# Entry of a gate and up stage: operand sums moved from GpSimd to VectorE, finer layer norm steps, two more early chunks

## The chip, the core and the metric

One NeuronCore of a Trainium2 chip runs the kernel. The metric is the device time in microseconds (us), as the median of several executions. The engines are called PE (TensorE), DVE (VectorE), ACT (ScalarE), POOL (GpSimd) and SP (SyncE); all transfers here are issued from SP's queue.

## The reference

One layer of a decoder on 1024 new prompt tokens and 8 sequences of 4 sample tokens, 1056 tokens in all, in fp32:

```python
m = W_out(concat[gated_delta_net_heads(x), sliding_window_attention_heads(x)])
x = layernorm(ALPHA * x + m)                       # layer norm 1
gate, up = split(x @ w_ffn_in)
x = layernorm(ALPHA * x + (silu(gate) * up) @ w_ffn_out)
```

The model width is 1024. The states and key and value caches are outputs too. The change touches the end of layer norm 1 and the first of the two products of the SwiGLU, here called the gate and up stage.

## The kernel before, in words

Activations lie transposed in SBUF: 8 tiles of 128 partitions (d = 0 to 7) by tokens, in two halves of 512 and 544 columns. An fp32 product is made of three matmuls on parts in fp32r: every operand is split into a high part, a copy by ACT, and a low part, the raw value minus the high part, by DVE. `product` (L1796 to L1798) runs wh·xh, wh·xl and wl·xh for four tiles. Weights are loaded in pieces of 128x512 (256 KB) and split at L161 (wh, ACT) and L162 (wl, DVE); four split pieces are held at a time.

The hidden width is 22 chunks (f = 0 to 21) of 128 gate and 128 up columns. A chunk is made by seven products in place of eight (the Strassen-Winograd scheme). Weights of a chunk are quarters A11, A12, A21, A22; operands are B11 and B21 (first half of the tokens, d 0 to 3 and d 4 to 7) and B12 and B22 (second half, 544 wide). With T1 = B12 - B11, T2 = B22 - T1, T3 = B22 - B12 and T4 = B21 - T2, and weight sums S1 to S4 that POOL makes for each chunk (L1625, L1626, L1630, L1636; tiles named S), PE runs in this order: A11·B11, S2·T2, A12·B21, S3·T3, A22·T4, S1·T1, S4·B22.

A11·B11 (`head`: ACT copies it out to x1 at L1857) and A12·B21 (`head2`: ACT's Silu to x2 at L1865) need only the first half. So the first NE = 10 chunks run these two products early, while the other engines finish the second half's layer norm 1 and the operands T. Eight of these chunks store x1 and x2 in DRAM and read them back when their turn comes. Then PE waits until all operands are there (`need(lambda: "T" in flags)`) and the loop over f runs the other products.

The second half's layer norm is two groups of 272 columns (named l11 and l12). It multiplies by 1/sigma at L1531 (DVE) or, for two tiles of each group, L1529 (POOL), applies weight and bias at L1532 (ACT), and splits B22 in pieces of 272 columns at once (L1694 and L1695). `combine` makes the sums for four tiles i: T1 on POOL (L1730), T3 on DVE (L1731), T2 in T1's place on DVE (L1735), T4 in T3's place on POOL (L1736), each split right after it.

The program is written as generators that hand over to each other (`spawn`, `pump`, `need`, `yield`). A scheduler with its own timeline then sets each engine's order, and every engine runs its list in order. A buffer taken from the pool is first written by a tiny memset on POOL (L228), which waits until the slot's last reader is done; POOL's list stands still until then.

## Time and profile before

| | |
|---|---|
| median of 3 runs | 1309.69 us (1306.21 to 1312.10) |
| profiled execution | 1308.84 us |
| its span | 1307.0 us |
| PE busy in the span | 1249.6 us (96%) |
| DVE, ACT, POOL busy | 887.3, 620.2, 393.4 us |
| chain that ended last | PE 79%, DVE 10%, ACT 3%, issue 3%, DMA 3%, POOL 2% |

The profile is of one execution, 0.85 us under the median; 1.84 us of it lie outside the span. Matmuls overlap, so a matmul's own duration (0.39 us for 512 columns) is longer than the distance from its start to the next one's start, and that distance is the price. Tile names in the rows are without buffer numbers: "T1raw" at L1735 is T2, "T3raw" at L1736 is T4, "x" at L1857 an x1 tile. The early chunks and the entry lie between 505 and 640 us, the loop over the chunks after that.

### The profile page before, as it was taken

To read this page: it belongs to the slowest core of one execution; us is meant where nothing else is said; L and a number is where in the kernel's file an instruction comes from. 1 tells how busy PE (TensorE), PEld (TensorE's weight loads), DVE (VectorE), ACT (ScalarE), POOL (GpSimd) and SP (SyncE) were. 2 spreads that over 40 slices of the span, in tenths; PEclk is the share of its full clock that TensorE was granted. 3 is DMA by queue.
4 is the path that set the end of the run, shared out by engine and by line. 5 is a ranking of instruction groups with operands and counts; after the bars stand their busy time and mean duration, and the time that the engine had idled before them with its cause. 6 is when DMAs were issued, how large, how long until landed. Compare 5 with 4: busy or idle time off the path is not lost.

```text
span 1307.0 us, 25072 instructions
## 1 busy us (share of the span) xinstructions
PE 1249.6 (96%) x8673; PEld 1126.6 (86%) x8673; DVE 887.3 (68%) x2040; ACT 620.2 (47%) x1376; POOL 393.4 (30%) x1207
## 2 busy tenths in 40 slices
PE   8999899989899998997899999999999999999996
PEld 6877689988899987985899999999999999788995
DVE  6787975887986777868856665555555765632674
ACT  7765644656755542577322223223333554622453
POOL 1009410205713133436744332332321112111210
PEclk9999999999999998998899999999999999999998
DMA  7431341242223545545454432222323886643461
GB/s 256 130 89 66 89 134 46 87 127 65 62 83 125 170 142 163 180 135 192 143 156 140 142 108 75 90 70 78 104 91 101 279 284 187 201 121 108 142 220 47
DMA packets 119103, 170.82 MB, mean 131 GB/s; under 512 B 20272, under 2 KB 50096, under 8 KB 118960
## 3 DMA queue, kind: packets, MB, share of 16 engines
q1 hardware_dynamic: 118976, 169.22, 41.3%
q8 instruction: 68, 1.11, 0.3%
q14 instruction: 59, 0.48, 0.1%
HBM read 138.44 MB, written 31.75 MB: 130 GB/s over the span
## 4 chain that ended last, share of the span: by engine, by line
PE 79%; DVE 10%; ACT 3%; issue 3%; DMA 3%; POOL 2%; SPq 0%; DVEq 0%; ACTq 0%; POOLq 0%
PE acc L427 6%; PE acc L428 6%; PE acc L426 6%; PE acc L1796 6%; PE acc L1797 6%; PE acc L1798 6%; PE acc L1967 6%; PE acc L1965 6%; PE acc L1966 6%; PE ms L1798 5%; PE ms L1796 5%; PE ms L1797 5%; DMA hr<-hd 1%; DVE wl L162 1%; DVE st L1063 1%
## 5 line engine op out<-in xcount | busy, mean ns | idle before, releaser
L162 DVE TENSOR_TENSOR wl<-wr,wh 128x512 fp32r<-128x512 f32 x330 | 242.2, 737 | 143.5 <-ACT wh L161 137.4
L161 ACT CAST wh<-wr 128x512 fp32r<-128x512 f32 x330 | 197.5, 602 | 261.2 <-PE acc L1966 104.2
L426 PE MATMUL acc<-xh,wh 128*128 128x272 f32 (+1 forms) x528 | 174.9, 331 | 6.0 <-ACT xh L345 5.2
L427 PE MATMUL acc<-xl,wh 128*128 128x272 f32 (+1 forms) x528 | 174.0, 330 | 0.0
L1967 PE MATMUL acc<-hx,wl 128*128 128x272 f32 (+1 forms) x528 | 171.8, 326 | 2.0 <-DVE wl L162 2.0
L428 PE MATMUL acc<-xh,wl 128*128 128x272 f32 (+1 forms) x528 | 173.6, 329 | 0.0
L1965 PE MATMUL acc<-hx,wh 128*128 128x272 f32 (+1 forms) x528 | 172.5, 327 | 1.0 <-ACT wh L161 1.0
L161 ACT CAST wh<-S 128x512 fp32r<-128x512 f32 x88 | 54.4, 619 | 148.0 <-PE acc L1797 96.3
L426 PEld LDWEIGHTS acc<-xh,wh 128*128 128x128 f32 x528 | 100.8, 191 | 13.2 <-ACT xh L345 5.2
L1967 PEld LDWEIGHTS acc<-hx,wl 128*128 128x128 f32 x528 | 99.9, 189 | 11.3 <-DVE wl L162 3.3
L1965 PEld LDWEIGHTS acc<-hx,wh 128*128 128x128 f32 x528 | 99.8, 189 | 9.7 <-POOL hx L228 1.2
L427 PEld LDWEIGHTS acc<-xl,wh 128*128 128x128 f32 x528 | 100.6, 191 | 8.6 <-issue 1.8
L428 PEld LDWEIGHTS acc<-xh,wl 128*128 128x128 f32 x528 | 100.8, 191 | 7.0 <-issue 0.2
L1966 PE MATMUL acc<-hx,wh 128*128 128x272 f32 x352 | 101.9, 290 | 0.0
L162 DVE TENSOR_TENSOR wl<-S,wh 128x512 fp32r<-128x512 f32 x88 | 71.3, 812 | 37.4 <-ACT wh L161 34.7
L1966 PE MATMUL acc<-hy,wh 128*128 128x512 f32 x176 | 69.5, 395 | 0.0
L1966 PEld LDWEIGHTS acc<-hx,wh 128*128 128x128 f32 x352 | 67.0, 191 | 0.3
L428 PE MATMUL acc<-mh,wl 128*128 128x272 f32 (+1 forms) x192 | 63.4, 330 | 0.0
L426 PE MATMUL acc<-mh,wh 128*128 128x272 f32 (+1 forms) x192 | 62.9, 328 | 0.0
L427 PE MATMUL acc<-ml,wh 128*128 128x272 f32 (+1 forms) x192 | 62.5, 326 | 0.0
L1694 ACT CAST hx<-hr 128x272 fp32r<-128x272 f32 (+1 forms) x66 | 31.5, 486 | 52.3 <-DMA hr<-hd 49.8
L1798 PE MATMUL ms<-T2h,wl 128*128 128x272 f32 x176 | 50.8, 289 | 0.0
(629 smaller groups left out, 3481.8 us busy)
## 6 DMA issues: line engine op xcount, KB each, us to landing
wr<-in_w_ffo_t SPq DMA_DIRECT2D x120, 256.0 KB, 2.9
wr<-in_w_ffi_t SPq DMA_DIRECT2D x108, 256.0 KB, 2.8
wr<-in_w_in_t SPq DMA_DIRECT2D x88, 256.0 KB, 2.7
wr<-in_w_out_t SPq DMA_DIRECT2D x32, 256.0 KB, 2.9
hd<-x SPq DMA_DIRECT2D x22, 272.0 KB, 2.8
hr<-hd SPq DMA_DIRECT2D x44, 136.0 KB, 2.7
hd<-x SPq DMA_DIRECT2D x22, 256.0 KB, 2.0
hr<-hd SPq DMA_DIRECT2D x22, 256.0 KB, 4.8
```

What stands on the lines that cost most here:

```text
L161: nc.scalar.copy(hi, raw)
L162: nc.vector.tensor_tensor(lo, raw, hi.bitcast(F32), ALU.subtract)
L426: mm(ps[:, :cw], wh, xh[kt][:, c0:c0 + cw], start=(kt == 0), stop=False)
L427: mm(ps[:, :cw], wh, xl[kt][:, c0:c0 + cw], start=False, stop=False)
L428: mm(ps[:, :cw], wl, xh[kt][:, c0:c0 + cw], start=False, stop=(kt == n - 1))
L1694: A.copy(hi, raw)
L1796: mm(o, wh[:, kt, :], xh, start=(start and kt == 0), stop=False, **kw)
L1797: mm(o, wh[:, kt, :], xl, start=False, stop=False, **kw)
L1798: mm(o, wl[:, kt, :], xh, start=False, stop=(kt == 3), **kw)
L1965: mm(ps, wh[:, f % 4, :], xh, start=(f == 0), stop=False)
L1966: mm(ps, wh[:, f % 4, :], xl, start=False, stop=False)
L1967: mm(ps, wl[:, f % 4, :], xh, start=False, stop=(f == NF - 1))
```

## The change

T1, T2 and T3 get a raw tile each and T4 is written over T2; all four subtractions are on DVE (now L1739, L1740, L1742, L1745), and T2 is made and split first; T3, T4, T1 and B22 are split behind it, with a flag each that the product which needs it waits for. B22 is no longer split in the layer norm but last in `combine`, in whole pieces of 544 columns. The layer norm of the second half hands over after every tile, puts all multiplies on DVE (L1533) and runs its steps with a longer lag (L1F). Twelve chunks are early: ten ahead of the loop as before, chunk 10 between S2·T2 and S3·T3 of chunk 0, and chunk 11 between S3·T3 and A22·T4. In the changed program the split of weights is L163 and L164, the copies to x1 and x2 are L1876 and L1884, and POOL's sums L1627, L1628, L1632 and L1638.

```diff
--- before.py
+++ after.py
@@ -78,11 +78,13 @@
     return c
 
 
-NE = 10
+NE = 12
+NBETWEEN = 2
 NKEEP_X = 2
 PM = (1, 4)
 MID = (1, 4)
 L1 = (0, 1)
+L1F = (1, 3)
 LE = 0
 BUDS = (2750.0, 3000.0)
 IDLE = (9, 4, 2, 3, 2, 4)
@@ -1466,7 +1468,7 @@
         hook(1)
 
 
-    def layernorm(tiles, ssum, cw, gi, nm, done, lag=(0, 0), sums=None, bk="acc", order=range(8)):
+    def layernorm(tiles, ssum, cw, gi, nm, done, lag=(0, 0), sums=None, bk="acc", order=range(8), fine=False):
 
 
         def ones_mm(src):
@@ -1502,7 +1504,7 @@
                 else:
                     G.tensor_tensor(v[0], v[0], q, ALU.add)
                 drop()
-            if i % 2 and not sums:
+            if (i % 2 or fine) and not sums:
                 yield 0.0
         drop(bk)
         if not sums:
@@ -1525,13 +1527,13 @@
         drop()
         for j, i in enumerate(order):
             t = tiles[i]
-            if j in PM:
+            if j in PM and not fine:
                 G.tensor_tensor(t, t, y, ALU.mult)
             else:
                 pin(V.tensor_tensor(t, t, y, ALU.mult))
             A.activation(t, t, AF.Identity, bias=cols[:, gi + 1, i:i + 1], scale=cols[:, gi, i:i + 1])
             done(i, t)
-            if j % 2:
+            if j % 2 or fine:
                 yield 0.0
         drop()
 
@@ -1643,9 +1645,12 @@
         return {"S2": (s2, first), "S3": (last("S3", f"S3_{f}"), third), "S1": (last("S1", f"S1_{f}"), None),
                 "S4": (last("S2", f"S2_{f}"), None)}
 
-    for f in range(NE):
+    def ahead(f):
         q = quarters(f)
-        plan[f] = {n: W.plain(W.raw(q[n])) for n in ("A11", "A12")}
+        plan.setdefault(f, {}).update({n: W.plain(W.raw(q[n])) for n in ("A11", "A12")})
+
+    for f in range(NE - NBETWEEN):
+        ahead(f)
     for f in range(NF):
         q, early = quarters(f), f < NE
         uses = {"A11": 2 - early, "A21": 1, "A22": 1, "A12": 2 - early}
@@ -1657,6 +1662,8 @@
                 p[n] = W.piece(*sm[n])
             elif n not in p:
                 p[n] = W.plain(r[n])
+            if f == 0 and n in ("S2", "S3"):
+                ahead(NE - 2 + (n == "S3"))
     wfo = I["w_ffo_t"]
     fo = {(g, d): W.whole(wfo[:, d * NF * P:(d + 1) * NF * P]) for g in range(len(GT)) for d in range(8)}
 
@@ -1701,13 +1708,13 @@
 
         def done(i, t):
             dma(out=yd[i][:, SG[s][0] + c0:SG[s][0] + c0 + cw], in_=t)
-            n = {(0, 0): "B11", (0, 1): "B21", (1, 1): "B22"}.get((s, i // 4))
+            n = {(0, 0): "B11", (0, 1): "B21"}.get((s, i // 4))
             if n:
                 split(*(x[:, cs] for x in B[n][i % 4]), t)
             flags.add(("y1", gi, i))
 
-        yield from layernorm([ac[s][d][:, cs] for d in range(8)], ssum, cw, 0, f"l1{gi}", done, L1, bk="acc" if gi else "ms",
-                             order=(0, 4, 1, 5, 2, 6, 3, 7) if s else range(8))
+        yield from layernorm([ac[s][d][:, cs] for d in range(8)], ssum, cw, 0, f"l1{gi}", done, L1F if s else L1,
+                             bk="acc" if gi else "ms", order=(0, 4, 1, 5, 2, 6, 3, 7) if s else range(8), fine=s)
         flags.add(("y1", gi))
 
     def pair(n, i, w, tags=("hp", "xp", "xs")):
@@ -1721,29 +1728,38 @@
 
     def combine():
 
+
+        raws = []
         for i in range(4):
             yield from wait(*[("y1", g, j) for g in range(3) for j in (i, 4 + i)])
             b11, b21, b12, b22 = ac[0][i], ac[0][4 + i], ac[1][i], ac[1][4 + i]
-            while not spare(8):
+            while not spare(5):
                 yield BLOCK
-            t1, t3 = (take([P, HW_], F32, f"{n}raw{i}") for n in ("T1", "T3"))
-            G.tensor_tensor(t1, b12, b11, ALU.subtract)
+            t1, t2, t3 = (take([P, HW_], F32, f"{n}raw{i}") for n in ("T1", "T2", "T3"))
+            V.tensor_tensor(t1, b12, b11, ALU.subtract)
+            V.tensor_tensor(t2, b22, t1, ALU.subtract)
+            yield 0.0
             V.tensor_tensor(t3, b22, b12, ALU.subtract)
-            split(*pair("T3", i, HW_), t3)
+            split(*pair("T2", i, HW_), t2)
             yield 0.0
-            split(*pair("T1", i, HW_), t1)
-            V.tensor_tensor(t1, b22, t1, ALU.subtract)
-            G.tensor_tensor(t3, b21, t1, ALU.subtract)
-            split(*pair("T2", i, HW_), t1)
+            V.tensor_tensor(t2, b21, t2, ALU.subtract)
+            raws.append((t1, t2, t3, b22))
+            drop("hp", 3)
             yield 0.0
-            give(f"T1raw{i}")
-            while not spare(2):
-                yield BLOCK
-            split(*(x[:, 0:512] for x in pair("T4", i, 512)), t3[:, 0:512])
-            give(f"T3raw{i}")
-            drop("hp", 4)
-            yield 0.0
-        flags.add("T")
+        flags.add("T2")
+        for n, j, w in (("T3", 2, HW_), ("T4", 1, 512), ("T1", 0, HW_), ("B22", 3, HW_)):
+            for i in range(4):
+                while not spare(2) and n != "B22":
+                    yield BLOCK
+                p = B[n][i] if n == "B22" else pair(n, i, w)
+                split(*(x[:, 0:w] for x in p), raws[i][j][:, 0:w])
+                if j < 3:
+                    give(f"T{j + 1}raw{i}")
+                else:
+                    drop()
+                if i % 2:
+                    yield 0.0
+            flags.add(n)
 
     def split_mix():
         for t in range(8):
@@ -1780,6 +1796,7 @@
 
 
     HALF = [(0, 272), (272, 544)]
+    filling = [1]
 
     def banks(tag, w):
         n = 1 if w == 512 else 2
@@ -1798,6 +1815,8 @@
                 mm(o, wl[:, kt, :], xh, start=False, stop=(kt == 3), **kw)
                 if c1 - c0 == 512 and kt == 1:
                     W.step()
+                    if filling:
+                        pump(BUD[0])
             if c1 == 272:
                 unit()
 
@@ -1867,13 +1886,16 @@
         unit()
 
     xd = [[k.dp.tile([P, w], F32, name=f"xd{f}_{w}") for w in (HW_, 512)] for f in range(NE)]
-    for f in range(NE):
+    def early(f):
         head(f)
         head2(f)
         if f >= NKEEP_X:
             for i in range(2):
                 dma(out=xd[f][i], in_=X[f][i])
                 give(f"x{i + 1}_{f}")
+
+    for f in range(NE - NBETWEEN):
+        early(f)
 
     def recall(f):
         if NKEEP_X <= f < NE:
@@ -1883,7 +1905,7 @@
             for i in range(2):
                 dma(out=X[f][i], in_=xd[f][i])
 
-    need(lambda: "T" in flags)
+    need(lambda: "T2" in flags)
     for f in range(NF):
         end = f == NF - 1
         p = plan[f]
@@ -1902,10 +1924,13 @@
         unit()
         if f >= NE:
             head2(f)
+        if f == 0:
+            early(NE - 2)
         if end:
             free("B21")
         while not spare(2):
             assert pump(), "no progress"
+        need(lambda: "T3" in flags)
         x3 = take([P, HW_], F32, f"x3_{f}")
         q = banks("acc", HW_)
         product(p["S3"], "T3", q)
@@ -1914,6 +1939,9 @@
         if end:
             free("T3")
         unit()
+        if f == 0:
+            early(NE - 1)
+        need(lambda: "T4" in flags)
         x4 = take([P, 512], F32, f"x4_{f}")
         q = banks("acc", 512)
         product(p["A22"], "T4", q)
@@ -1926,12 +1954,16 @@
         if end:
             free("T4")
         unit()
+        need(lambda: "T1" in flags)
         q = banks("ms", HW_)
         product(p["S1"], "T1", q)
         evac(q, lambda ps, c: V.tensor_tensor(x3[:, c], x3[:, c], ps, ALU.add))
         if end:
             free("T1")
         unit()
+        if f == 0:
+            need(lambda: "B22" in flags)
+            filling.clear()
         product(p["S4"], "B22", q, start=False)
         evac(q, lambda ps, c: V.tensor_tensor(x1[:, c], x1[:, c], ps, ALU.add))
         drop("ms", 2)
```

DVE's list ahead of wl138, the low part of the weights of the last early A11·B11, before (wl137 and wl138 are weights, T1l and T3l low parts of operands, T1raw at L1735 is T2):

```order
L162 TENSOR_TENSOR wl137_8110<-wr137_7779,wh137_8109 128x512
L1695 TENSOR_TENSOR T1l0_7923<-T1raw0_7872,T1h0_7921 128x544
L1695 TENSOR_TENSOR B22l2_6871<-mx16_4283,B22h2_6869 128x272
L1695 TENSOR_TENSOR T3l1_8027<-T3raw1_8021,T3h1_8025 128x544
L1695 TENSOR_TENSOR T1l1_8058<-T1raw1_8019,T1h1_8056 128x544
L1735 TENSOR_TENSOR T1raw0_7872<-mx14_3540,T1raw0_7872 128x544
L162 TENSOR_TENSOR wl138_8149<-wr138_7804,wh138_8148 128x512
```

and in the changed program, from wl137 to wl139, which belongs to the last early A12·B21 ahead of the loop:

```order
L164 TENSOR_TENSOR wl137_8098<-wr137_7783,wh137_8097 128x512
L1740 TENSOR_TENSOR T2raw1_7929<-mx15_3721,T1raw1_7927 128x544
L1702 TENSOR_TENSOR B22l3_6875<-mx17_4468,B22h3_6873 128x544
L1739 TENSOR_TENSOR T1raw2_8000<-mx12_4571,ac2_6355 128x544
L1742 TENSOR_TENSOR T3raw2_8004<-mx16_4283,mx12_4571 128x544
L164 TENSOR_TENSOR wl138_8149<-wr138_7808,wh138_8148 128x512
L1702 TENSOR_TENSOR T3l1_8111<-T3raw1_7931,T3h1_8109 128x544
L1702 TENSOR_TENSOR T2l1_7962<-T2raw1_7929,T2h1_7960 128x544
L1533 TENSOR_TENSOR mx13_4747<-mx13_4747,l11y_7812 128x272
L1533 TENSOR_TENSOR mx13_4747<-mx13_4747,l12y_7818 128x272
L1740 TENSOR_TENSOR T2raw2_8002<-mx16_4283,T1raw2_8000 128x544
L164 TENSOR_TENSOR wl139_8198<-wr139_7857,wh139_8197 128x512
```

Behind wl137 stand 5 instructions of DVE up to wl138 before, and 4 now, of which three are subtractions; splits of T1 are gone from this stretch, and the first splits of tile 1 of T2 and T3 stand behind wl138. One split of T3 further on comes wl140, the low part of S2 of chunk 0; before, three instructions stood between wl139 and wl140.

POOL's list from S2 of chunk 0 (L1626) on, before (T3raw at L1736 is T4, x1_8 is the buffer of an early product, S3_0 the next weight sum):

```order
L1626 TENSOR_TENSOR S2_0_8144<-S1_0_8142,wr140_7896 128x512
L228 MEMSET T2h2_8169 128x1
L1736 TENSOR_TENSOR T3raw0_7874<-ac4_6535,T1raw0_7872 128x544
L228 MEMSET T2l2_8171 128x1
L1736 TENSOR_TENSOR T3raw1_8021<-ac5_6632,T1raw1_8019 128x544
L228 MEMSET x1_8_8177 128x1
L1854 MEMSET x1_8_8177 128x32
L228 MEMSET S3_0_8187 128x1
L228 MEMSET T4h2_8207 128x1
L228 MEMSET T4l2_8209 128x1
L1630 TENSOR_TENSOR S3_0_8187<-wr140_7896,wr141_7951 128x512
```

and in the changed program from S2 (L1628) to the same buffer x1_8:

```order
L1628 TENSOR_TENSOR S2_0_8144<-S1_0_8142,wr140_7905 128x512
L230 MEMSET T4h0_8154 128x1
L230 MEMSET T4l0_8156 128x1
L230 MEMSET T4h1_8160 128x1
L230 MEMSET T4l1_8162 128x1
L230 MEMSET T4h2_8173 128x1
L230 MEMSET T4l2_8175 128x1
L230 MEMSET T4h3_8179 128x1
L230 MEMSET T4l3_8181 128x1
L1638 TENSOR_TENSOR S2_0_8144<-wr143_8038,S2_0_8144 128x512
L230 MEMSET x1_8_8187 128x1
L1873 MEMSET x1_8_8187 128x32
```

Two subtractions of 128x544 have gone from between S2 and x1_8; the sum S4 (L1638), and six more memsets than stood there before, are ahead of x1_8 now.

PE's list at the first products with T2, before (wh140 and wl140 are the parts of S2 of chunk 0; B21 with wh137 is an early product of chunk 8):

```order
L1796 MATMUL ms_8313<-T2h0_7929,wh140_8221 128x272
L1796 MATMUL ms_8314<-T2h0_7929,wh140_8221 128x272
L1797 MATMUL ms_8313<-T2l0_7931,wh140_8221 128x272
L1797 MATMUL ms_8314<-T2l0_7931,wh140_8221 128x272
L1796 MATMUL acc_8180<-B21h0_6845,wh137_8109 128x512
L1797 MATMUL acc_8180<-B21l0_6847,wh137_8109 128x512
L1798 MATMUL acc_8180<-B21h0_6845,wl137_8110 128x512
```

and in the changed program (B11 with wh141 is the early product of chunk 10):

```order
L1813 MATMUL ms_8319<-T2h0_7887,wh140_8242 128x272
L1814 MATMUL ms_8319<-T2l0_7889,wh140_8242 128x272
L1813 MATMUL ms_8320<-T2h0_7887,wh140_8242 128x272
L1814 MATMUL ms_8320<-T2l0_7889,wh140_8242 128x272
L1813 MATMUL acc_8354<-B11h0_6829,wh141_8279 128x512
L1814 MATMUL acc_8354<-B11l0_6831,wh141_8279 128x512
L1815 MATMUL ms_8319<-T2h0_7887,wl140_8243 128x272
L1813 MATMUL ms_8319<-T2h1_7960,wh140_8242 128x272
L1814 MATMUL ms_8319<-T2l1_7962,wh140_8242 128x272
L1815 MATMUL ms_8319<-T2h1_7960,wl140_8243 128x272
L1813 MATMUL ms_8319<-T2h2_8016,wh140_8242 128x272
L1815 MATMUL ms_8320<-T2h0_7887,wl140_8243 128x272
```

The first T2 matmuls stand at the same place of the list. Before, the early product of chunk 8 follows them at once; now it comes behind T2's second and third tile and the start of chunk 10.

## Rows read from the trace of the kernel before

**Rows 1.** Busy time by stretch of 20 us: stretch, length, engines busy, PEclk, DMA share, GB/s.

```profile
600.00:620.00 20.00, 13.30 (x47) 9.82 (x46) 18.85 (x25) 13.99 (x29) 13.86 (x16) 0.84 0.51 174
620.00:640.00 20.00, 16.27 (x77) 13.94 (x77) 16.85 (x15) 9.10 (x16) 16.99 (x35) 0.82 0.37 125
640.00:660.00 20.00, 20.00 (x148) 19.30 (x147) 16.50 (x29) 5.47 (x9) 10.97 (x22) 1.00 0.61 187
```

**Rows 2.** Waits of PE from 596 to 645: total us, times, longest us.

```profile
PE acc L1798 <- DVE wl L162: 5.9, 2, 4.3
PE acc L1796 <- ACT x L1857: 4.4, 2, 3.7
PE acc L1796 <- ACT wh L161: 0.8, 1, 0.8
```

**Rows 3.** Timeline of PE, 599 to 625: start, us, line, operation, idle before it.

```profile
599.40 0.50 PE L1796 MATMUL acc<-B21h,wh 128*128 128x512 f32 x1 [0.65 <-ACT x L1857]
...
605.55 0.50 PE L1798 MATMUL acc<-B11h,wl 128*128 128x512 f32 x1 [1.54 <-DVE wl L162]
...
606.34 0.39 PE L1798 MATMUL acc<-B11h,wl 128*128 128x512 f32 x1
606.57 0.39 PE L1796 MATMUL acc<-B11h,wh 128*128 128x512 f32 x1
...
615.70 0.80 PE L1798 MATMUL acc<-B11h,wl 128*128 128x512 f32 x1 [4.33 <-DVE wl L162]
...
617.14 0.63 PE L1798 MATMUL acc<-B11h,wl 128*128 128x512 f32 x1
617.57 0.63 PE L1796 MATMUL acc<-B11h,wh 128*128 128x512 f32 x1
...
620.13 0.61 PE L1796 MATMUL ms<-T2h,wh 128*128 128x272 f32 x2
...
624.72 0.80 PE L1796 MATMUL acc<-B21h,wh 128*128 128x512 f32 x1 [3.73 <-ACT x L1857]
```

**Rows 4.** Timeline of POOL, 593 to 624.

```profile
593.58 4.35 POOL L1529 TENSOR_TENSOR mx<-mx,l12y 128x272 f32<-128x272 f32 x2 [4.39 <-DVE l12y L1524]
...
615.12 7.08 POOL L1736 TENSOR_TENSOR T3raw<-ac,T1raw 128x544 f32<-128x544 f32 x1 [3.84 <-DVE T1raw L1735]
...
622.20 1.33 POOL L1736 TENSOR_TENSOR T3raw<-ac,T1raw 128x544 f32<-128x544 f32 x1
623.47 0.09 POOL L228 MEMSET x<- 128x1 f32 x1
...
623.74 1.47 POOL L1630 TENSOR_TENSOR S<-wr,wr 128x512 f32<-128x512 f32 x1
```

**Rows 5.** Timeline of DVE, 598 to 626.

```profile
598.40 0.69 DVE L162 TENSOR_TENSOR wl<-wr,wh 128x512 fp32r<-128x512 f32 x1 [1.83 <-ACT wh L161]
...
606.93 0.78 DVE L1531 TENSOR_TENSOR mx<-mx,l12y 128x272 f32<-128x272 f32 x2
607.63 0.71 DVE L1731 TENSOR_TENSOR T3raw<-mx,mx 128x544 f32<-128x544 f32 x1
...
614.96 0.68 DVE L162 TENSOR_TENSOR wl<-wr,wh 128x512 fp32r<-128x512 f32 x1
...
622.88 2.87 DVE L1695 TENSOR_TENSOR T4l<-T3raw,T4h 128x512 fp32r<-128x512 f32 x2 [1.87 <-ACT T4h L1694]
625.88 1.63 DVE L162 TENSOR_TENSOR wl<-S,wh 128x512 fp32r<-128x512 f32 x1
```

**Rows 6.** Timeline of ACT, 593 to 626.

```profile
593.12 1.28 ACT L1865 ACT_TABLE_LOAD   x1
...
624.08 0.58 ACT L1857 COPY x<-acc 128x512 f32<-128x512 f32 x1
```

**Rows 7.** DMA issues: count, KB each, median us to landing.

```profile
xd<-x SPq DMA_DIRECT2D x8, 272.0 KB, 2.1
...
x<-xd SPq DMA_DIRECT2D x8, 272.0 KB, 3.4
```

## Prediction

> **What bounds the kernel now.** I read the stretches first, then PE's waits there, then the timelines of the engines that PE waited for. From 640 on PE is busy for the whole of its 20 us at full clock, though it has nothing to spare for a better order of other engines. The two stretches before it are not like that: 13.30 and 16.27 us of 20, at a mean granted clock of 0.84 and 0.82 [rows 1]. This is the entry that the change rewrites, so the question is how much of what is lost there comes back.
>
> PE waits there 5.9 us for low parts of weights from DVE, 4.4 for x1 copies of ACT and 0.8 for a high part of weights, 11.1 together [rows 2]. The timeline gives the places: 0.65 at 599.40 and 1.54 at 605.55, between them the 0.8 for the high part, then 4.33 at 615.70 (wl138, the last early A11·B11) and 3.73 at 624.72 (the copy of x1_8, ahead of the A12·B21 of chunk 8). Ahead of 606 a 512-column matmul starts 0.23 after the one before (606.34 to 606.57). After the wait of 4.33 the distance is 0.43 (617.14 to 617.57), so the clock has fallen to its lower level, 1.2 in place of 2.4 GHz; the three short waits did not do that [rows 3]. Ten such matmuls follow 615.70 and twelve follow 624.72, each 0.20 too long: 4.4 us. The entry thus loses 11.1 + 4.4 = 15.5 us, which is the most that a perfect entry could give.
>
> Why were the two late? The wait for wl138 is DVE's list: from wl135 at 598.40 it needed until 614.96 for the instructions ahead of wl138, and part of that time POOL was subtracting. The prices where POOL is quiet are 0.71 for 544 columns, 0.39 for 272 and 0.68 for a weight; beside a POOL sum a weight took 1.63 [rows 5]. The x1 copy was late because of POOL's list: a T4 subtraction begun at 615.12 took 7.08 us, the next one 1.33, and only then came the memset of the x buffer at 623.47 [rows 4], ACT's copy at 624.08 [rows 6] and PE at 624.72 [rows 3].
>
> **The change part by part.**
>
> *VectorE.* It takes over 8 subtractions of 544 columns (T1, T4), 8 x 0.71 = 5.7 us, and 4 multiplies of 272, 4 x 0.39 = 1.6; B22's low parts go from 8 narrow to 4 wide ones, about even. What it is rid of is POOL beside it: eight sums and four multiplies (one pair took 4.35 us [rows 4]). A DVE instruction beside one costs about 1.63 - 0.68 = 0.95 more [rows 5], so at least 8 x 0.95 = 7.6 go. The work as a whole comes out even; the order is what counts. Between wl135 and wl138 the new list has ten instructions of 544 columns, two of 272 and two weights: 10 x 0.71 + 2 x 0.39 + 2 x 0.68 = 9.2 us. So wl138 starts near 598.4 + 0.7 + 9.2 = 608.3, 6.6 earlier than at 614.96, which is more than the 4.33 that PE waited. Up to wl140 come wl138, wl139, four of 544 and two of 272, 5.0 us more: 613.3.
>
> *PE.* It came to the first T2 product at 620.13, after waits of 0.65, 0.8, 1.54 and 4.33 and ten slow matmuls. Without these it is there at 620.13 - 7.3 - 2.0 = 610.8. Four T2 matmuls and two of chunk 10 (about 1 us) stand ahead of the first that needs wl140, so PE waits about 1.5 us for it. If S1 and S2 of chunk 0 on POOL each slow one instruction of DVE by 0.95, it is 3.4; if instructions overlap as their starts suggest (607.63 against 606.93 for two), nothing. I take 1.5, since the lists hold no more.
>
> *Order of need and two more chunks between.* Before, PE went through T2 tile by tile, as DVE finished, with one early product as cover. Now it has chunk 10's and 11's four products of 12 x 0.23 = 2.8 us, 11 us in all, to put between S2·T2, S3·T3 and A22·T4, while DVE needs 0.71 for each further split. T2's last tile and the tiles of T3 and T4 then come ahead of PE or within a us of it; T1 and B22 have more time. I cost these at nothing; without that cover T3's four splits alone would be 2.8 us.
>
> *Layer norm.* Its two Rsqrt steps come together, which saves two table loads of 1.28 us on ACT [rows 6]. ACT works ahead of PE by little there, so this pays for later affine steps that now wait on DVE alone. Net nothing, between -1.3 and +1.3.
>
> *POOL.* Its list at the entry now holds S1, S2, S4 and memsets. The memset for x1_8 stands behind S4, at 1.33 to 1.47 each [rows 4] plus memsets that wait for stores to DRAM, 2.1 us from issue to landing [rows 7]. The three x1 copies there I cost at a wait of 0.65 each, as at 599.40 [rows 3]; the lower end is 0, the upper one 3.73.
>
> *Transfers.* Two chunks more are stored and read back: four transfers out and four in, landing in 2.1 and 3.4 us [rows 7], and four weights of 256 KB are loaded twice. They are issued on SP with the others, in stretches where the DMA engines are 0.37 to 0.61 busy [rows 1]. Their cover is the loop with its eight slots of weights; without cover the first recalled chunk would cost its 3.4 us once.
>
> *Sum.* Left over: 3 x 0.65 for copies, 0.8 for a high part of weights, 1.5 for wl140, 1.5 for one more low part as at 605.55, together 5.8 us, none long enough to drop the clock by the three short ones above [rows 3]. The gain is 15.5 - 5.8 = 9.7. On the profiled execution of 1308.84 that is 1299.1; its median of 1309.69 is 0.85 higher, so 1300.0. I say 1299.5.
>
> **A rule against a row.** The T4 sum at 615.12 took 7.08 us although its like took 1.33 right after [rows 4]: DVE's list ran on from 614.96 and first stood still at 621.0, 1.87 ahead of 622.88 [rows 5], and POOL was done 1.2 after that. Taken as typical, each of POOL's weight sums beside an unbroken DVE list costs up to 7.08 - 1.33 = 5.75 us more, and the time is that of the first rival. The Trainium skill, "SBUF — State Buffer", section "Who interferes with whom", says that a VectorE instruction with two SBUF inputs contends with a GpSimd instruction that reads SBUF, and that whoever issues first holds the ports for that whole instruction while the other waits. By that a sum would wait for one DVE instruction, 1.33 + 0.71 = 2.0 us, and 1299.5 would stand; the row of 7.08 disagrees, the weight of 1.63 agrees.
>
> **The rivals.**
>
> *POOL's sums starve.* For it: 615.12, and the new DVE list has no gap up to wl140. Against it: sums of 1.47 at 623.74 beside DVE work [rows 4]. S1 and S2 are then made only when DVE stands at wl140, at 612.6: 2 x 1.33 for them, 0.6 for the cast, as for the copy at 624.08 [rows 6], so PE waits from 610.8 to 615.9 and 0.7 more for wl140, 5.8 instead of 1.5, and the next twelve matmuls at half clock add 2.4. That is 6.7 worse: 1306.
>
> *ACT becomes the bound.* It runs casts, affine steps and copies in one list, and the high parts of T2 now come earlier in it, behind copies that wait for PE. If x1 copies and wh140 wait 1.5 to 2 us each in place of 0.65, four of them give 4 to 5 back: 1304.
>
> *The whole stall goes.* Everything arrives in time and no wait is left: 1309.7 - 15.5 = 1294. Against it: three short waits of today lie ahead of what the change touches.
>
> *Slower.* The starving hits the chain that the x1 memset ends, too: S4 held as at 615.12, with x1_8 behind it, then S3. Each costs 5.75 and 2.4 for the clock, 8.1; two of them beyond the forecast give 1316, three 1324; I name 1318. It decides once what is lost in the entry is over 15.5 + 6.5 = 22 us. Against it: DVE itself stands still at wl140 and lets POOL through.
>
> *The change doesn't do what it says.* The chunks between may not cover: the list already has chunk 11's second product behind the first half of S1·T1. Then PE waits for T3 or T4 up to 2.8 us, 1302, which lies in the forecast's range.
>
> **How the numbers follow.** Forecast 0.50 (1296 to 1304), no stall left 0.10, starving 0.22, ACT 0.10, slower 0.08. About 0.5%, 6.5 us, is what a measurement of this kernel can tell from no change: faster is below 1303.1, slower above 1316.2. Faster takes 0.46 of the forecast, all 0.10 of the case without a stall, and 0.05 each of the starving and the ACT case: 0.66. Slower is 0.08, the rest 0.26. The range from 1292 to 1309 takes in all but the upper end of the starving case and the slower case.
>
> **What would show it.** Right: in the stretches 600 to 640 PE busy for 17 us or more of 20, no idle time of over 2 us, distances of 0.23 throughout, wl138 some 6 us earlier, no POOL sum above 2 us. Starving: S1 or S2 of chunk 0 at 3 us or more, and PE waiting for wh140. ACT: PE's waits name L1876. The prediction is wrong if the entry's waits are gone and the time still stands, since then the loss comes back later, in the loop or at the recalled chunks.

## The result and the profile after

The changed kernel takes 1300.02 us (median of 12 runs, 1295.20 to 1302.57), the kernel before 1308.02 (12 runs): a ratio of 0.994, 95% interval 0.9927 to 0.9953. That is 8.0 us faster, where the prediction said 1299.5 and, against the median it had, 10.2 us.

The two stretches of the entry and the one after it, in the windows view of the changed kernel (columns as in [rows 1]):

```profile
600.00:620.00 20.00, 15.05 (x61) 12.30 (x60) 16.18 (x26) 10.66 (x21) 11.87 (x29) 0.83 0.44 145
620.00:640.00 20.00, 19.99 (x106) 17.06 (x106) 13.62 (x20) 9.02 (x17) 7.16 (x20) 1.00 0.65 215
640.00:660.00 20.00, 20.00 (x146) 19.20 (x145) 12.66 (x20) 5.48 (x9) 10.19 (x18) 1.00 0.48 153
```

PE is busy for 35.04 of the 40 us after 600, where it was 29.57 [rows 1]. The stretch that was the second bad one is whole now. The first still has a gap and a clock of 0.83. PE's waits from 596 to 645 in the changed kernel:

```profile
PE ms L1813 <- ACT wh L163: 3.1, 1, 3.1
PE acc L1813 <- ACT wh L163: 1.8, 1, 1.8
PE acc L1813 <- ACT x L1876: 0.5, 1, 0.5
```

They add to 5.4 us (5.5 by the timeline), where [rows 2] had 11.1. None is for a low part any more, and the wait for x1 copies has gone from 4.4 to 0.5. What is left is for high parts, cast by ACT. PE's timeline:

```profile
597.97 0.50 PE L1813 MATMUL acc<-B21h,wh 128*128 128x512 f32 x1 [0.51 <-ACT x L1876]
...
609.17 0.39 PE L1813 MATMUL ms<-T2h,wh 128*128 128x272 f32 x1 [3.12 <-ACT wh L163]
609.40 0.29 PE L1814 MATMUL ms<-T2l,wh 128*128 128x272 f32 x1
...
611.77 0.79 PE L1813 MATMUL acc<-B11h,wh 128*128 128x512 f32 x1 [1.83 <-ACT wh L163]
...
616.34 0.63 PE L1813 MATMUL acc<-B21h,wh 128*128 128x512 f32 x1
616.76 0.63 PE L1814 MATMUL acc<-B21l,wh 128*128 128x512 f32 x1
...
618.17 0.39 PE L1815 MATMUL acc<-B21h,wl 128*128 128x512 f32 x1
618.40 0.40 PE L1813 MATMUL acc<-B21h,wh 128*128 128x512 f32 x1
```

PE reaches the first T2 product at about 606 and starts it at 609.17. Four matmuls later it stops again for 1.83 us, and then a 512-column matmul starts 0.42 or 0.43 after the one before, until 618: the lower clock, as in [rows 3] after the 4.33. From 611.77 to 617.94 stand 9 matmuls of 512 columns and 10 of 272. At 0.23 and 0.127 they would need 3.3 us; they took 6.2, so 2.8 is clock. The waits and this together cost 8.3 us, half of the 15.5 that the prediction read from the kernel before.

Behind the wait of 3.12 stands one instruction of ACT, and behind that one of POOL. ACT's cast of S2 and of the next weight, POOL's sums and VectorE's list, all of the changed kernel:

```profile
608.50 0.62 ACT L163 CAST wh<-S 128x512 fp32r<-128x512 f32 x1 [5.38 <-POOL T4l L230]
...
611.11 0.61 ACT L163 CAST wh<-wr 128x512 fp32r<-128x512 f32 x1
```

```profile
600.17 0.10 POOL L230 MEMSET x<- 128x1 f32 x1 [0.66 <-DMA xd<-x]
...
600.38 6.71 POOL L1627 TENSOR_TENSOR S<-wr,wr 128x512 f32<-128x512 f32 x1
...
607.21 1.26 POOL L1628 TENSOR_TENSOR S<-S,wr 128x512 f32<-128x512 f32 x1
...
609.93 1.68 POOL L1638 TENSOR_TENSOR S<-wr,S 128x512 f32<-128x512 f32 x1 [1.18 <-DVE wl L164]
```

```profile
599.53 0.72 DVE L1702 TENSOR_TENSOR B22l<-mx,B22h 128x544 fp32r<-128x544 f32 x1
...
601.44 0.69 DVE L164 TENSOR_TENSOR wl<-wr,wh 128x512 fp32r<-128x512 f32 x1
...
605.26 0.71 DVE L1702 TENSOR_TENSOR T3l<-T3raw,T3h 128x544 fp32r<-128x544 f32 x1
609.15 0.69 DVE L164 TENSOR_TENSOR wl<-S,wh 128x512 fp32r<-128x512 f32 x1 [3.18 <-ACT wh L163]
...
610.40 1.76 DVE L1702 TENSOR_TENSOR T4l<-T2raw,T4h 128x512 fp32r<-128x512 f32 x1
```

S1 begins at 600.38 and takes 6.71 us, S2 then 1.26, the cast 0.62. (The row of the cast names a memset that POOL ran in the same instant; S2's end, at 608.47, is what the cast needs.) VectorE runs from before 599.53 to 605.97 without a gap and then stands still for 3.18 us, waiting for the cast. POOL's sum ends at 607.09, 1.1 us after VectorE stopped, which is about the time that such a sum takes alone. The 1.83 us behind it are an echo: ACT had stood still for 5.38 us ahead of the cast of S2 and had a cast, two affine steps and another cast in its list before the next weight, at 611.11. The rows agree with a sum that made no headway while VectorE was busy, as the T4 subtraction of [rows 4] did. Here such a sum is said to starve.

But most sums beside a busy VectorE do not starve. S4, in the rows above, begins at 609.93 in a list that runs from 609.15 to 619.08 without a gap and takes 1.68 us; it is VectorE's next instruction, at 610.40, that is held, 1.76 us in place of 0.68. It was the same in the kernel before. There VectorE's list had no gap from 602.31 to 621.01; four of POOL's sums that began in it between 603 and 610 took 1.55 to 1.79 us each, and only the T4 subtraction at 615.12 starved. One of the four, and the VectorE instruction beside it:

```profile
607.95 1.55 POOL L1625 TENSOR_TENSOR S<-wr,wr 128x512 f32<-128x512 f32 x1
```

```profile
608.27 1.82 DVE L1695 TENSOR_TENSOR T3l<-T3raw,T3h 128x544 fp32r<-128x544 f32 x1
```

**What a profiled execution can be compared by.** The changed kernel's profiled execution took 1295.20 us, the fastest of its twelve, so the two spans differ by 13.6 us and not by 8. In the tile view, first and last start of the matmuls on B11 (first early product) and on hx (first matmul behind the gate and up stage), before:

```profile
L1796 PE MATMUL acc<-B11h,wh x88: 387/393/628, 557.9 to 1002.7; 128*128 128x512 f32 x88
...
L1965 PE MATMUL acc<-hx,wh x528: 283/290/591, 1020.9 to 1289.9; 128*128 128x272 f32 x117, 128*128 128x512 f32 x59
```

and after:

```profile
L1813 PE MATMUL acc<-B11h,wh x88: 387/393/792, 553.3 to 990.5; 128*128 128x512 f32 x88
...
L1997 PE MATMUL acc<-hx,wh x528: 283/288/594, 1008.8 to 1276.1; 128*128 128x272 f32 x117, 128*128 128x512 f32 x59
```

From the first early product to the first matmul behind the stage it is 463.0 before and 455.5 after: 7.5 us less, close to the 8.0 of the medians. Of the rest, 4.6 us lie ahead of the stage, where PE has the same order in both programs, and vary from one execution to the next: the first early product started between 553.3 and 563.3 in the fourteen profiles read here. The table below uses this length of the stage beside the median.

### The profile page after: what moved, and what is told of

Read it like the earlier page. It is cut to its first block, busy times and chain, and to the rows that moved or that the text cites. A ratio compares the mean times of both kernels' runs of the same rounds, so it can differ in the third digit from the quotient of the medians.

```text
span 1293.4 us, 25107 instructions
## 1 busy us (share of the span) xinstructions
PE 1246.2 (96%) x8673; PEld 1123.6 (87%) x8673; DVE 879.3 (68%) x2048; ACT 616.8 (48%) x1370; POOL 371.7 (29%) x1203
## 4 chain that ended last, share of the span: by engine, by line
PE 75%; DVE 12%; ACT 4%; DMA 4%; issue 3%; POOL 1%; SPq 1%; DVEq 0%; ACTq 0%; POOLq 0%
PE acc L1813 6%; PE acc L1814 6%; PE acc L1999 6%; PE acc L1815 6%; PE acc L1998 6%; PE acc L1997 6%; PE acc L429 5%; PE acc L430 5%; PE acc L428 5%; PE ms L1815 5%; PE ms L1813 5%; PE ms L1814 5%; DVE wl L164 2%; DVE st L1065 2%; DMA hr<-hd 1%
## 5 line engine op out<-in xcount | busy, mean ns | idle before, releaser
L164 DVE TENSOR_TENSOR wl<-wr,wh 128x512 fp32r<-128x512 f32 x330 | 243.1, 740 | 141.1 <-ACT wh L163 136.6
L163 ACT CAST wh<-wr 128x512 fp32r<-128x512 f32 x330 | 197.5, 602 | 252.6 <-PE acc L1998 104.7
L163 ACT CAST wh<-S 128x512 fp32r<-128x512 f32 x88 | 54.5, 619 | 162.8 <-PE acc L1814 94.1
L164 DVE TENSOR_TENSOR wl<-S,wh 128x512 fp32r<-128x512 f32 x88 | 66.9, 760 | 39.4 <-ACT wh L163 36.4
L1813 PE MATMUL ms<-T2h,wh 128*128 128x272 f32 x176 | 51.2, 292 | 3.1 <-ACT wh L163 3.1
```

What stands on the lines that cost most here:

```text
L163: nc.scalar.copy(hi, raw)
L164: nc.vector.tensor_tensor(lo, raw, hi.bitcast(F32), ALU.subtract)
L1813: mm(o, wh[:, kt, :], xh, start=(start and kt == 0), stop=False, **kw)
```

## The experiments

| kernel | median us | ratio to before | 95% interval | stage us | longest sum on POOL in the entry |
|---|---|---|---|---|---|
| before | 1308 to 1309 | 1 | | 463.0 | T4, 7.08 |
| changed | 1300.02 | 0.994 | 0.9927 to 0.9953 | 455.5 | S1, 6.71 |
| e5, subtractions on VectorE alone | 1303.37 | 0.9965 | 0.9949 to 0.9982 | 457.8 | S1, 8.41 |
| e10, finer steps alone | 1315.38 | 1.0059 | 1.0039 to 1.008 | 470.7 | T4, 3.52 |
| e21, finer steps, more handing over | 1305.20 | 0.9992 | 0.9976 to 1.0008 | 463.2 | T1, 2.54 |
| e20, e21 and subtractions on VectorE | 1302.22 | 0.9961 | 0.9947 to 0.9975 | 458.7 | S1, 4.00 |
| e2, changed, T1 and T4 on POOL | 1303.38 | 0.996 | 0.9945 to 0.9975 | 457.0 | T1, 5.22 |
| e3, changed, no chunks in between | 1299.61 | 0.9926 | 0.9904 to 0.9949 | 453.4 | S1, 6.70 |
| e4, changed, coarse layer norm | 1306.03 | 0.9975 | 0.996 to 0.999 | 460.4 | S1, 5.86 |
| e12, changed, four multiplies on POOL | 1302.58 | 0.9954 | 0.9937 to 0.9972 | 457.0 | S1, 8.25 |
| e1, changed, S1 and S2 on VectorE | 1298.23 | 0.9928 | 0.9906 to 0.995 | 455.7 | S4, 6.45 |
| e9, e3 and S1, S2, S4 on VectorE | 1298.62 | 0.9931 | 0.9913 to 0.9949 | 454.4 | S3, 5.91 |
| e14, changed, S1 to S4 on VectorE | 1297.08 | 0.9923 | 0.9902 to 0.9944 | 450.6 | none over 1.9 |
| e18, e14, twelve early chunks ahead | 1293.75 | 0.9886 | 0.9865 to 0.9908 | 448.8 | none over 1.9 |

S1 to S4 in this table and below are those of chunk 0; "longest sum" is read from POOL's timeline between 580 and 650. Each ratio is to the kernel before as it ran beside that kernel.

### e1: two weight sums on VectorE

```diff
-            G.tensor_tensor(t["S1"], a["A21"], a["A22"], ALU.add)
-            G.tensor_tensor(t["S2"], t["S1"], a["A11"], ALU.subtract)
+            (V if f == 0 else G).tensor_tensor(t["S1"], a["A21"], a["A22"], ALU.add)
+            (V if f == 0 else G).tensor_tensor(t["S2"], t["S1"], a["A11"], ALU.subtract)
```

> The changed kernel with S1 and S2 of chunk 0 made on VectorE, not on GpSimd. Theory (GpSimd's first weight sum starves behind VectorE's unbroken list: S1 took 6.71 us, and PE then idled 3.12 and 1.83 us and ran some 2.8 us long at half clock): PE's wait for the high part of S2 falls from 3.12 to 1 or 2 us, the clock stays up, and the time is 3 to 6 us under the changed kernel's 1300, some 1295, ratio to before 0.990. Rival (VectorE is the bound itself, two more instructions only make it later): PE waits 3 us or more for the low part of S2 in place of the high one, and the time stays at 1300, ratio 0.994.

Measured 0.9928, 1.8 us under the changed kernel and not clear of it; the theory's 3 to 6 us did not come. PE's wait for S2 fell to 1.97 us as the theory has it, and the clock was 1.00 from 600 to 620, but a new wait came. PE's and POOL's timelines:

```profile
614.12 0.36 PE L1813 MATMUL ms<-T2h,wh 128*128 128x272 f32 x1 [1.97 <-POOL x L1873]
...
626.56 0.58 PE L1813 MATMUL acc<-B21h,wh 128*128 128x512 f32 x1 [4.18 <-ACT x L1876]
```

```profile
617.30 6.45 POOL L1638 TENSOR_TENSOR S<-wr,S 128x512 f32<-128x512 f32 x1
```

Now S4 is the sum that starves, with 6.45 us. The memsets of T1's and x1's buffers stand behind it; ACT's list stood still 4.75 us for a buffer of T1, with the copy to x1 behind it, and PE waited 4.18 for that copy. The starving moved on to the next sum in POOL's list. The rival (the low part of S2 late instead) did not come.

### e2: subtractions T1 and T4 back on GpSimd

```diff
-            V.tensor_tensor(t1, b12, b11, ALU.subtract)
+            G.tensor_tensor(t1, b12, b11, ALU.subtract)
...
-            V.tensor_tensor(t2, b21, t2, ALU.subtract)
+            G.tensor_tensor(t2, b21, t2, ALU.subtract)
```

> The changed kernel with the subtractions T1 and T4 back on GpSimd. Theory (their place on VectorE is the main part of the gain): they take 1.4 to 7 us each again beside VectorE, PE idles 6 us or more from 600 to 640, time 1304 to 1308, ratio to before 0.997 to 1.0. Rival (the order of need and the chunks in between carry the gain): T2's chain has cover either way, and the time stays within 1.5 us of 1300, ratio 0.994.

Measured 0.996, 3.4 us above the changed kernel in the medians, though the two intervals overlap; a little under the theory's 1304 and outside the rival's 1.5 us. PE and POOL:

```profile
602.06 0.50 PE L1815 MATMUL acc<-B11h,wl 128*128 128x512 f32 x1 [1.31 <-DVE wl L164]
...
612.64 0.80 PE L1815 MATMUL acc<-B11h,wl 128*128 128x512 f32 x1 [4.74 <-DVE wl L164]
```

```profile
603.74 5.22 POOL L1739 TENSOR_TENSOR T1raw<-mx,ac 128x544 f32<-128x544 f32 x1 [1.39 <-ACT mx L1534]
...
630.22 3.65 POOL L1745 TENSOR_TENSOR T2raw<-ac,T2raw 128x544 f32<-128x544 f32 x1 [0.50 <-DVE T2l L1702]
```

T1 takes 5.22 us and a T4 3.65; PE waits for low parts again, 1.31 and 4.74, as before.

### e3: no chunks in between

Ten early chunks, and the lines that plan and call the two in between left out.

```diff
-NE = 12
-NBETWEEN = 2
+NE = 10
+NBETWEEN = 0
...
-        if f == 0:
-            early(NE - 2)
...
-        if f == 0:
-            early(NE - 1)
```

> The changed kernel with ten early chunks and none in between. Theory (the gain is VectorE's list ahead of the first T2 product): the time stays at 1300 to 1302, ratio 0.994 to 0.996; the waits for S3 and T3 grow by no more than 2 us. Rival (the two chunks' 11 us of early products cover T2's last tile, T3 and T4): PE waits 3 to 6 us for splits of T2, T3 or T4 and the clock drops, 1304 to 1307, ratio 0.997 to 0.9995.

Measured 0.9926: the same as the changed kernel or a little better, so the two chunks in between bring nothing. PE's waits from 596 to 645:

```profile
PE ms L1811 <- ACT wh L163: 3.1, 1, 3.1
PE acc L1811 <- ACT x L1874: 0.5, 1, 0.5
```

The wait for S2's high part is the same 3.1 us, and no wait for T2, T3 or T4 came up: VectorE is far enough ahead without that cover.

### e4: the layer norm's coarse steps

```diff
-        yield from layernorm([ac[s][d][:, cs] for d in range(8)], ssum, cw, 0, f"l1{gi}", done, L1F if s else L1,
+        yield from layernorm([ac[s][d][:, cs] for d in range(8)], ssum, cw, 0, f"l1{gi}", done, L1,
...
-                             bk="acc" if gi else "ms", order=(0, 4, 1, 5, 2, 6, 3, 7) if s else range(8), fine=s)
+                             bk="acc" if gi else "ms", order=(0, 4, 1, 5, 2, 6, 3, 7) if s else range(8))
```

> The changed kernel with the coarse layer norm steps of before, four multiplies on GpSimd among them. Theory (these steps give little): within 2 us of 1300, ratio 0.993 to 0.9955. Rival (the layer norm's early end starts VectorE's list earlier, which is what brings wl138 forward): the first T1 comes 3 us later or more, PE waits for it, 1304 or more, ratio 0.997 or more.

Measured 0.9975, 6 us of the gain gone. The rival's time came, by another place than either had named. PE's timeline:

```profile
575.25 1.25 PE L1476 MATMUL acc<-l11var,ones_r 128*128 128x272 f32 x2 [4.14 <-DVE l11var L1511]
```

The product that sums the squares stands so early in PE's list that PE waits 4.14 us for its input. From 560 to 580 PE is busy for 15.86 us of 20 at a granted clock of 0.84; the changed kernel has 20.00 and 1.00 there. So has the kernel before, with the same coarse steps: what this run has in addition is the extra handing over described at e20, so the loss belongs to the two together.

### e5 and e10: one part alone

e5 puts T1 and T4 of the kernel before on VectorE (G to V in L1730 and L1736). e10 gives the kernel before the finer layer norm, its lag and its multiplies on VectorE.

> The kernel before with the subtractions T1 and T4 on VectorE and nothing else changed. Theory (VectorE beside a quiet GpSimd is worth much by itself): the T4 subtraction of 7.08 us and the sums of 1.8 us go, PE's 3.73 us wait for the x1 copy is gone, 3 to 6 us faster, ratio 0.995 to 0.998. Rival (it pays only with the early end of the layer norm and the order of need): 5.7 us more work stand in VectorE's list ahead of T2, the waits for low parts grow as much as the x1 wait shrinks, ratio 0.998 to 1.002.

> The kernel before with the finer layer norm steps, the longer lag and all its multiplies on VectorE, and nothing else changed. Theory (these steps pay only with the subtractions on VectorE, since without them GpSimd still slows VectorE's list): ratio 0.998 to 1.002. Rival (they carry most of the gain by themselves, as the loss of 6 us without them suggests): 5 us faster or more, ratio 0.996 or less.

e5: 0.9965, 4.7 us faster, as the theory said: by the medians, the subtractions' place is more than half of the gain by itself. PE's longest wait for an x1 copy is 0.7. POOL's list then has S1 next to VectorE's unbroken work, the longest such sum of all:

```profile
604.24 8.41 POOL L1625 TENSOR_TENSOR S<-wr,wr 128x512 f32<-128x512 f32 x1
```

e10: 1.0059, slower by 7 us; both expectations fell. The windows show where: the loss spreads over 60 us, with PE at 15.77, 13.55 and 17.35 of 20 and a granted clock of 0.74 in the middle.

```profile
600.00:620.00 20.00, 15.77 (x68) 12.15 (x66) 18.06 (x30) 15.99 (x30) 8.30 (x18) 0.92 0.57 195
620.00:640.00 20.00, 13.55 (x57) 11.27 (x57) 18.06 (x27) 11.76 (x22) 11.01 (x24) 0.74 0.15 51
640.00:660.00 20.00, 17.35 (x102) 15.56 (x102) 17.52 (x27) 4.32 (x8) 10.89 (x19) 0.83 0.38 109
```

### e12: four multiplies back on GpSimd

```diff
-            if j in PM and not fine:
+            if j in PM:
```

> The changed kernel with four of the layer norm's multiplies back on GpSimd, the finer steps and the lag kept. Theory (the steps and the lag matter, not the engine of the multiplies): within 2 us of the changed kernel's 1300, ratio 0.9925 to 0.9955. Rival (the multiplies beside VectorE's list, 4.35 us for a pair before, are what delays the layer norm): 1304 or more, ratio 0.997 or more.

Measured 0.9954, 2.6 us above the changed kernel with overlapping intervals: between the theory's 1302 and the rival's 1304, and not decided.

### e20 and e21: finer steps with more handing over

A finer step does less, so the same number of hand-overs brings the layer norm less far. The changed kernel has an extra one in each 512-column product until all operands are there; e10 had not. e21 is e10 with it, e20 also with the subtractions on VectorE.

```diff
+    filling = [1]
...
                 if c1 - c0 == 512 and kt == 1:
                     W.step()
+                    if filling:
+                        pump(BUD[0])
...
     need(lambda: "T" in flags)
+    filling.clear()
```

> The kernel before with the finer layer norm steps and the extra handing over in 512-column products, subtractions on GpSimd as before. Theory (the finer steps alone were 0.6% slower because each product let only one small step through, so operands came later; with the extra handing over they are as early as before, and GpSimd's subtractions still starve): 1303 to 1310, ratio 0.996 to 1.001. Rival (finer steps are slower without VectorE's subtractions whatever the handing over): 1313 or more, ratio 1.004 or more.

> The kernel before with the subtractions on VectorE, the finer layer norm steps and the extra handing over in 512-column products until the operands are there, but with the old order (T1, T3, T2, T4, one flag, B22 in the layer norm) and ten early chunks. Theory (the order of need and the late B22 give little; subtractions and steps are the change): 1298 to 1302, ratio 0.9925 to 0.9955, as the run without chunks in between. Rival (the order of need is a part of the gain): T2's last tile comes some 3 us later and PE waits for it, 1303 to 1307, ratio 0.996 to 0.999.

e21: 0.9992, no difference from before. (Eight of its runs lie below 1307 and four near 1310, so its median says less than its interval.) The finer steps were slow in e10 for want of hand-overs; with them they are worth nothing by themselves. e20: 0.9961, as e5 and short of e3's 0.9926 (the intervals meet at 0.9947 to 0.9949). From e21 to e20 only the subtractions move, and the intervals just fail to meet. What e3 has over e20 is the order of need with a flag for each product, a raw tile of its own for T2, the late split of B22, and hand-overs until then. e20's rows show what the old order costs, ACT's timeline and PE's:

```profile
615.86 0.62 ACT L1695 CAST T4h<-T3raw 128x512 fp32r<-128x512 f32 x1 [0.57 <-DVE T3raw L1737]
616.38 0.58 ACT L1861 COPY x<-acc 128x512 f32<-128x512 f32 x1
```

```profile
617.01 0.80 PE L1798 MATMUL acc<-B21h,wh 128*128 128x512 f32 x1 [5.73 <-ACT x L1861]
```

ACT's list has the cast of a T4 tile, for which it waits on VectorE, ahead of the copy of x1; PE waits 5.73 us for that copy. The rival's ratio came, but not its wait for T2's last tile. That the order of need is part of the gain, 2.6 us in the medians and 5.3 in the stage's length with the finer steps in place, is likely and not clear of noise.

### e9, e14 and e18: no sum of chunk 0 on GpSimd

e9 is e3 with S1, S2 and S4 of chunk 0 on VectorE; e14 the changed kernel with all four; e18 is e14 with the twelve early chunks all ahead of the loop (NE = 12, NBETWEEN = 0 and the calls in between left out, as in e3).

> The changed kernel without the two chunks in between (ten early ones) and with S1, S2 and S4 of chunk 0 on VectorE. Theory (what is left of the entry's loss is GpSimd's sums starving, S1 with 6.71 us in the changed kernel and S4 with 6.45 us where S1 and S2 alone were moved): no GpSimd sum above 3 us, PE idle below 3 us from 600 to 640, no half clock, 1294 to 1298, ratio to before 0.988 to 0.992. Rival (VectorE is the bound then): PE waits 4 us or more for low parts of S2, T3 or T4, 1299 to 1303, ratio 0.993 to 0.996.

> The changed kernel with all four weight sums of chunk 0 on VectorE. Theory (a sum on GpSimd starves while VectorE's list has no gap, and whichever of them is next in the list is the one: S1 in the changed kernel, S4 with S1 and S2 moved, S3 with S4 moved too; with none left nothing starves): no GpSimd sum above 3 us between 590 and 640, PE idle below 4 us there, no half clock, 1293 to 1297, ratio to before 0.987 to 0.991. Rival (four more instructions on VectorE cost what they save): PE waits 3 us or more for low parts or for S2's high part, 1297 to 1300, ratio 0.992 to 0.994.

> The changed kernel with all twelve early chunks ahead of the first T2 product, none in between, and the four weight sums of chunk 0 on VectorE. Theory (11 us more of early products let VectorE get to T2 and S2 before PE does): PE idle below 3 us from 590 to 650, 1292 to 1297, ratio to before 0.986 to 0.991. Rival (VectorE only gets as much more to do, and GpSimd's sums of chunk 1 starve next): PE waits at the later products of chunk 0 or at chunk 1, 1298 or more, ratio 0.992 or more.

e9 missed: 0.9931, no better than e3. By the ratio that is the start of the rival's range, but the waits below are not for low parts. POOL and PE:

```profile
613.96 5.91 POOL L1632 TENSOR_TENSOR S<-wr,wr 128x512 f32<-128x512 f32 x1
```

```profile
620.57 0.39 PE L1811 MATMUL acc<-T3h,wh 128*128 128x272 f32 x1 [3.58 <-ACT wh L163]
```

S3 was the one sum left on POOL in the entry, and it starved, 5.91 us; PE waited 3.58 for the cast of it. In e14 no sum of chunk 0 is left on POOL to starve. Its windows and PE's waits from 590 to 645:

```profile
600.00:620.00 20.00, 17.55 (x77) 13.69 (x76) 19.60 (x35) 18.14 (x36) 1.84 (x23) 0.99 0.68 228
620.00:640.00 20.00, 20.00 (x103) 17.18 (x102) 18.68 (x27) 10.31 (x20) 6.43 (x23) 0.93 0.52 172
```

```profile
PE ms L1813 <- POOL x L1873: 1.9, 1, 1.9
PE acc L1813 <- ACT x L1876: 0.5, 1, 0.5
```

POOL's busy time falls to 1.84 and 6.43 us and PE idles 2.4 us, though the clock still fell once, to 0.93 as a mean of the second stretch, which the theory had ruled out. The wait of 1.9 is once more for the high part of S2. The view names a memset of POOL, but ACT's cast is what comes just ahead of it, and the cast waits for VectorE, which makes S2 at 616.43:

```profile
617.20 0.62 ACT L163 CAST wh<-S 128x512 fp32r<-128x512 f32 x1 [1.23 <-DVE S L1628]
```

The time is 1297.08, ratio 0.9923: just outside the theory's range and inside the rival's, while the wait of 3 us that the rival asked for did not come. It is better than the changed kernel by 2.9 us with overlapping intervals. e18 is clear of it. Its windows, and PE's waits from 590 to 660:

```profile
600.00:620.00 20.00, 18.38 (x77) 13.85 (x76) 20.00 (x35) 16.93 (x34) 2.13 (x29) 1.00 0.62 204
620.00:640.00 20.00, 20.00 (x119) 17.86 (x119) 16.31 (x24) 7.99 (x15) 7.13 (x20) 1.00 0.67 228
```

```profile
PE acc L1811 <- ACT x L1874: 1.0, 2, 0.5
PE acc L1813 <- DVE wl L164: 0.6, 1, 0.6
```

PE idles 1.6 us in all, each time for 0.6 or less, and the clock is 1.00 in both stretches. At 1293.75 us, ratio 0.9886, it is 14.4 us faster than before, and 6 faster than the changed kernel, with intervals that don't meet. Nearly all of the 15.5 us is back. No run has the twelve chunks ahead with the sums left on POOL, so this gain is not divided between the two.

## Why the prediction was right, and where its steps were not

*The number and the mechanism.* The time lies in the forecast's range, but that 1300.02 is only half a microsecond from 1299.5 is luck: the kernel before measured 1308.02 beside it, 1.7 under the 1309.69 that the forecast started from, and the gain was smaller by about as much. By the signs that the prediction named, the mechanism is half the forecast's and half a rival's. wl138 came early and the second stretch is whole; but PE is busy for 15.05 us of the first 20, idles 3.12 at once and runs a while at the lower clock. Both signs of starving are there, S1 above 3 us and PE waiting for wh140.

*The loss and its ceiling.* 15.5 us was the sum of waits and clock read from [rows 2, 3]. e18 gets 14.4 of it back in the median and 14.2 in the stage's length (463.0 to 448.8). This step held.

*VectorE's list ahead of wl138.* Right: no wait for a low part is left in the changed kernel, and wl138 is the row at 601.44. This execution's stage began 4.6 us earlier than that of before (553.3 and 557.9), so 601.44 stands for 606.0 there: 9 us earlier than 614.96, where 6.6 were forecast. PE's arrival at the first T2 product, 606.1 or 610.7 in the other's time, is the 610.8 of the forecast. That arrival counted the short waits of 0.65, 0.8 and 1.54 as gone, while the sum kept them as left over; the runs bear out the arrival. The subtractions' move alone is worth 4.7 us (e5); undoing it costs 3.4 (e2, not clear of noise).

*The x1 copies.* Costed at three waits of 0.65; one of 0.51 came.

*S2 and wl140.* Here the sum was off. I took 1.5 for a low part, 1.5 for another, and 0.8 for a high part, with no drop of the clock. Low parts cost nothing; two high parts cost 3.12 and 1.83, and the clock 2.8. The cause is the one I gave 0.22: S1 starved behind VectorE's unbroken list, 6.71 us as against 7.08 in [rows 4]. It cost 7.8 us in all, near the rival's 8.2 (5.8 for the waits and 2.4 for the clock). The first wait was shorter than the rival's, since VectorE came to wl140 at 605.97, 610.6 in the time of before and not 612.6; the echo of 1.83 was not in the rival's sum. What kept the time in the forecast's range is the rest: for copies, a high part and a low part I had left 1.95, 0.8 and 1.5, and only 0.5 came. So the forecast's 5.8 us for what is left became 8.3, and the gain 7.5 to 8.0 in place of 9.7.

*Layer norm, costed at nothing between -1.3 and +1.3.* Wrong as a step. With everything else in place the coarse steps cost 6 us (e4); by themselves the finer ones are worth nothing (e21) or cost 7 (e10). They are tied to how often the program hands over and cannot be priced alone; I had counted their instructions and not their place in PE's list.

*Two chunks in between.* I costed the order of need at nothing thanks to their cover. The cover wasn't needed: e3 without them is no slower, and no wait for T3 or T4 shows. Put ahead of the first T2 product instead, the same two chunks are worth some 3 us on top of e14's sums on VectorE (e18; the two intervals overlap slightly).

*The rule.* The Trainium skill, "SBUF — State Buffer", section "Who interferes with whom", calls the ports that VectorE shares with GpSimd an exclusive lock, and has issue order decide which of the two waits; by that, the later of two such instructions waits for one whole instruction of the other engine. The traces agree where VectorE is the one that waits: its split of a weight took 1.63 in place of 0.68 beside a POOL sum [rows 5], and the 1.76 and 1.82 above are of the same kind. They disagree for the sums that starve: within S1's 6.71 us VectorE started nine instructions. An estimate by the rule gives S1 some 2 us and has it done at 602.4, S2 at 604.4, and PE would not have waited 3.12 at 606. What decides whether a sum starves stays open: the two that starved in [rows 4] and in the changed kernel began 0.16 and 0.22 us into an instruction of VectorE's list, and S4, which did not, 0.17 into one.

## What to carry to other kernels

A two-input sum on GpSimd that starts while VectorE has an unbroken list of two-input work takes a little longer than alone in most cases, but now and then it is done only when that list stops; so don't leave one on a path that VectorE's own list, or PE, will wait for. Moving one sum off GpSimd let the next one in its list starve (e1, e9): move all that stand in the stretch. And put cover ahead of the wait, where it gives the slow engines time, not behind it; e18 suggests this, against e14 and e3.

## What the runs showed of the hardware

The length of a starving sum was set by VectorE, not by the sum. In eleven of the fourteen kernels a sum of 512 or 544 columns, 1.3 us when alone, took 3.5 to 8.4 us in the entry. In ten of the eleven its longest one was done 1.1 to 1.2 us after VectorE's list stopped; in e20 it was done 1.1 us after a pause of 0.03 us in that list. Starving is the rarer case: of the 71 sums of this size that POOL began between 590 and 645 us in the fourteen profiles, with VectorE's list running on for 2.5 us or more, sixty took 1.3 to 1.8 us and eleven 2.7 or more.

The granted clock of the changed kernel fell to its lower level at 611.0, inside the wait of 1.83 and 1.8 us after PE had started again behind the wait of 3.12, and it came back at 617.8. Which of the two waits brought it is not shown: in e9 it fell 1.4 us after a wait of 3.58 had ended, in e14 1.5 us after one of 1.94, and in e1 it did not fall in the 12 us after one of 1.97. In e18, with waits of 0.6 and less, it stayed at 1.00.

The part of the kernel ahead of the entry varies by up to 10 us between executions, as the start of the first early product shows; the spans of one profile of each kernel would have put the gain at 13.6 us.
